# A two-layer hybrid backbone: HGRN's columns first in the input projection, its recurrence beside RWKV's columns

## The chip, the cores and the metric

The kernel runs on one NeuronCore of a Trainium2 chip. Its engines have a queue each: TensorE (PE, with its weight loads PEld), VectorE (DVE), ScalarE (ACT), GpSimd (POOL) and SyncE (SP), which issues most of the DMAs. Matrix products land in PSUM, everything else lies in SBUF. The metric is the device time of one execution in microseconds.

## The reference

One sample of 512 latent tokens and 256 context tokens, model width 1024, two layers. A layer normalises, projects all tokens to the columns of four mixers, joins their outputs in one projection, and ends in a feed-forward block (dense in layer 0, top 2 of 8 experts in layer 1). Cut to the mixers of this change:

```python
h = rms_norm(x) * (1 + scale) + shift
p_hgrn, p_rwkv, p_swa, p_mla = split_cols(h @ w_in[l], GROUP_COLS)

# HGRN2, both directions; chunks of 64 tokens, state S per head
q, zf, zb, i, g = split_cols(p_hgrn, (256,) * 5)
f = lb[d] + (1 - lb[d]) * sigmoid(z);  key = (1 - lb[d]) * sigmoid(-z)
def step(S, inp):                       # gla_chunked, one chunk
    inter = (q * exp(b)) @ S            # b: running sum of log f in the chunk
    att[t, s] = sum_k q[t, k] * key[s, k] * exp(b[t, k] - b[s, k])   # s <= t
    o = inter + att @ i
    S = exp(b_end) * S + (key * exp(b_end - b)).T @ i

# RWKV-7, both directions, a step per token
sa = S @ kk_t
S = S * w_t - sa * b_t + v_t * k_t;  o_t = S @ r_t
```

Each direction starts with the context tokens and goes on over the latents. In layer 1 the context's outputs are not needed.

## The kernel before

The function `mixers` is traced once for each layer and has the stages that matter here.

*Input projection.* The normalised tokens `hhi`, `hlo` (768 tokens, channels on partitions) are multiplied by 23 tiles of 128 columns and by a token-major group (`proj_tok`). Every product takes three passes of split float32 operands (lines 272 to 274). The weights of half a column come by DMA into `raww` and are split by ACT (`hiw`) and DVE (`low`). A column is accumulated in one of three PSUM tiles `big`. The order of the columns is written out: the nine of RWKV (`RW_COLS`) first, then `rw_prep` (decays, keys, values: everything that needs no state, with small products in two PSUM banks `sml`), then HGRN's eight columns, its gates (`hg_gates`), `proj_tok`, and six columns of the attentions, which are spilled to DRAM (`spill`). Ahead of the last three of these `rw_first` prepares the operands of RWKV's first pair of chunks.

*Recurrences.* Python generators are traced side by side by `weave`, which takes a given number of steps of each in turn: `rw_dir` for RWKV's two directions (1 step a round each), `hgrn` for both directions of HGRN (0.44 steps in layer 0, 0.36 in layer 1), `attention_prep` (0.5), and in layer 0 modulation vectors. There are some 122 rounds. RWKV works on pairs of 64-token chunks, six pairs to a direction: `rw_pair` makes their operands (AR, BK), the masked products G and the inverse of a triangular matrix by doubling (TU, TP, AP), and `rw_chain` carries the state Z. HGRN works on segments of four chunks, three to a direction: a segment scales keys and queries by decays (dd, XQ, QE), makes its products level by level into `att`, carries the state `sa`, and writes its output, all through two PSUM banks `hg`. When HGRN's first direction is done, `attention_prep` loads the spilled columns over its inputs.

A list scheduler orders the instructions of each engine by their priority in this trace; memory comes from pools, and a tile of a pool that opens later waits for the one whose place it takes.

Of the kernel before, what the change touches and what calls it, by code (L numbers as in the profile page):

```python
# [23 lines left out]
T = LAT + CTX  # L24
# [10 lines left out]
# columns of the per-layer parameter block  # L35
# [4 lines left out]
# columns of the constant block  # L40
# [7 lines left out]
def _consts():  # L48
    """Constants that depend on shapes alone."""
# [54 lines left out]
def _col_tiles():  # L104
    """Column tiles (lists of w_in columns) that are computed channels x tokens, and the token-major group."""
# [17 lines left out]
# heads 0, 2, 1, 3  # L123
# [6 lines left out]
def _pack(inp):  # L130
# [7 lines left out]
    # shifts and scales of two channel tiles side by side  # L138
# [84 lines left out]
class Ker:  # L223
# [19 lines left out]
    def weave(*gens):  # L243
        """Traces several streams side by side: (generator, steps at a time)."""
# [31 lines left out]
    def gemm_col(s, ps, parts, act, segs):  # L276
        """ps[:, tokens] = weights^T act for one tile of 128 output channels.  parts: (first k, tiles) of the weights."""
# [7 lines left out]
    def gemm_last(s, m, *a):  # L285
        """Column m; the last one a segment after the other, as the norm of the first begins beside the second."""
# [3 lines left out]
    def gemm_cols(s, cols, act, ks=range(KT)):  # L290
        """The same for several column tiles (psum, parts, segments) together, k by k."""
# [8 lines left out]
    def diag(s, out, lhsT, rhs, start=True, stop=True):  # L300
        """64 x 64 products of the two partition halves, each with its own half."""
# [3 lines left out]
    def dtrans(s, out, x, idm):  # L305
        """64 x 64 transposes of the two partition halves."""
# [35 lines left out]
    def setup(s):  # L342
# [5 lines left out]
        s.cst = per.tile([128, C_MSK], F32, name="cst")  # L348
        s.prm = per.tile([128, L, NPRM], F32, name="prm")
        s.cT = per.tile([128, KT, 2], F32, name="cT")  # L350
        s.mskf = per.tile([128, 2, 6, 64], F32, name="mskf")
# [9 lines left out]
        s.mg = s.cst[:, C_MG:C_MG + 512].rearrange("p (d q n) -> p d q n", d=2, q=2)  # L361
# [17 lines left out]
    def setup_masks(s):  # L379
        """The constants that the recurrences need."""  # L380
        Q, V = s.Q, s.V
        Q.dma_start(s.cst[:, C_BO:], s.I['cst'][:, C_BO:C_MSK])
        for l in range(1, L):
            Q.dma_start(s.prm[:, l], s.I['prm'][l])
        Q.dma_start(s.mskf, s.I['cst'][:, C_MSK:C_MSK + 768].rearrange("p (d h n) -> p d h n", d=2, h=6))
        V.tensor_copy(s.msk, s.mskf)
        V.tensor_add(s.id2, s.idn[:, :64], s.idn[:, 64:])
        # masks of the pairs that hold the diagonal as well
        mdf = s.acc[:, :128].rearrange("p (d n) -> p d n", d=2)
        for d in range(2):  # L390
            V.tensor_add(mdf[:, d], s.mskf[:, 1 - d, 0], s.id2)
        V.tensor_copy(s.mdg, mdf)

# [1577 lines left out]
```

## Time and profile before

| | |
|---|---|
| median of 3 runs | 2641.1 us (2638.34 to 2641.53) |
| span of the profiled execution | 2644.5 us; its own time isn't listed beside it, and the span stands 0.13% above the median |
| mean granted TensorE clock | 0.961 of full speed |
| PE, DVE, ACT, POOL busy | 91%, 63%, 46%, 18% of the span |
| layer 0: projection, recurrences | 63 to 288.6 us, 288.6 to 580.2 us |
| layer 1: projection, recurrences | 1395 to 1599 us, 1599 to 1847 us |

The four stretches are those that the change touches; the rest of the span is the norms, the mixers' readout, the output projection and the feed-forward blocks. A busy share of an engine is told by stage, as the stages have different limits. PEclk is the TensorE clock that the throttle granted.

### The profile page before, as it was taken

The numbers are of one execution on the slowest core, as the hardware profiler recorded it, in microseconds if no ns is written. First come the engines' busy times: TensorE is split into PE (matmuls) and PEld (weight loads), VectorE is DVE, ScalarE is ACT, GpSimd is POOL, SyncE is SP. The second block draws the span as 40 slices with busy tenths as digits, with TensorE's granted clock in tenths as the row PEclk, the third lists the DMA queues.
The fourth block names the chain that finished last, engine by engine and source line by source line (L and its number), as shares of the span: only waits on it lengthen the run. The fifth ranks groups of instructions, "written<-read, shape, count | busy, mean of one in ns | idle before, by whom it ended". The sixth has DMA issues, their size and how long they took to land. (4 is left out here: it accounts for less than half of the span.)

```text
span 2644.5 us, 46379 instructions
## 1 busy us (share of the span) xinstructions
PE 2408.1 (91%) x18131; PEld 1998.6 (76%) x18131; DVE 1660.6 (63%) x3055; ACT 1227.3 (46%) x2331; POOL 484.9 (18%) x613
## 2 busy tenths in 40 slices
PE   6999788879998999999999997888996999999994
PEld 3889666656586888888888786666674898899993
DVE  5573598777578644344336746876745667667765
ACT  4373356546723211211234654664653556555653
POOL 1010464441011000000020005654102000000002
PEclk9999899989998999999999998998998899999997
DMA  6223110111053433334322130001113888888885
GB/s 245 65 89 111 49 34 20 30 65 57 1 178 129 144 112 120 117 116 132 118 81 64 57 116 13 20 16 49 56 36 107 267 270 270 280 265 264 260 277 179
DMA packets 161026, 322.46 MB, mean 122 GB/s; under 512 B 12288, under 2 KB 84736, under 8 KB 160800
## 3 DMA queue, kind: packets, MB, share of 16 engines
q1 hardware_dynamic: 153744, 293.60, 34.2%
q0 software_dynamic: 6480, 23.73, 2.5%
q8 instruction: 144, 2.36, 0.4%
q10 hardware_dynamic: 576, 2.10, 0.2%
q14 instruction: 82, 0.67, 0.1%
HBM read 295.39 MB, written 22.54 MB: 120 GB/s over the span
## 5 line engine op out<-in xcount | busy, mean ns | idle before, releaser
L272 PE MATMUL big<-hhi,hiw 128*128 128x512 f32 (+1 forms) x1504 | 520.8, 347 | 9.1 <-ACT hhi L491 4.6
L273 PE MATMUL big<-hlo,hiw 128*128 128x512 f32 (+1 forms) x1504 | 523.6, 348 | 2.4 <-DVE hlo L492 2.4
L274 PE MATMUL big<-hhi,low 128*128 128x512 f32 (+1 forms) x1504 | 519.5, 346 | 5.8 <-DVE low L260 3.9
L259 ACT CAST hiw<-raww 128x512 fp32r<-128x512 f32 (+3 forms) x208 | 158.4, 769 | 616.9 <-PE big L273 413.4
L272 PEld LDWEIGHTS big<-hhi,hiw 128*128 128x128 f32 x1504 | 286.2, 191 | 53.2 <-ACT hhi L491 5.7
L274 PEld LDWEIGHTS big<-hhi,low 128*128 128x128 f32 x1504 | 286.2, 190 | 45.1 <-DVE low L260 5.6
L273 PEld LDWEIGHTS big<-hlo,hiw 128*128 128x128 f32 x1504 | 286.4, 190 | 41.0 <-DVE hlo L492 4.2
L260 DVE TENSOR_TENSOR lom<-rawm,him 128x1024 fp32r<-128x1024 f32 x176 | 215.1, 1225 | 128.0 <-ACT him L259 126.7
L260 DVE TENSOR_TENSOR low<-raww,hiw 128x512 fp32r<-128x512 f32 (+3 forms) x196 | 177.3, 909 | 161.1 <-ACT hiw L259 160.8
L259 ACT CAST him<-rawm 128x1024 fp32r<-128x1024 f32 x176 | 184.3, 1047 | 150.4 <-PE sml L273 60.7
L272 PE MATMUL sml<-xh,him 128*128 128x256 f32 x528 | 152.0, 288 | 0.0
L273 PE MATMUL sml<-xl,him 128*128 128x256 f32 x528 | 149.5, 283 | 0.0
L274 PE MATMUL sml<-xh,lom 128*128 128x256 f32 x528 | 149.4, 283 | 0.0
L260 DVE TENSOR_TENSOR lov<-rawv,hiv 128x1024 fp32r<-128x1024 f32 x88 | 107.5, 1222 | 38.2 <-ACT hiv L259 37.8
L272 PE MATMUL sml<-him,xh 128*128 128x256 f32 x440 | 127.4, 290 | 0.7 <-DVE xl L260 0.6
L273 PE MATMUL sml<-lom,xh 128*128 128x256 f32 x440 | 125.4, 285 | 0.0
L274 PE MATMUL sml<-him,xl 128*128 128x256 f32 x440 | 125.3, 285 | 0.0
L273 PE MATMUL big<-gl,hiw 128*128 128x512 f32 (+1 forms) x352 | 119.5, 339 | 0.0
L272 PE MATMUL big<-gh,hiw 128*128 128x512 f32 (+1 forms) x352 | 118.9, 338 | 0.0
L274 PE MATMUL big<-gh,low 128*128 128x512 f32 (+1 forms) x352 | 118.2, 336 | 0.0
L259 ACT CAST hiv<-rawv 128x1024 fp32r<-128x1024 f32 x88 | 92.4, 1050 | 51.3 <-PE y L274 41.5
L757 POOL TENSOR_TENSOR Gm<-G,mskf 128x256 f32<-128x256 f32 x120 | 99.5, 836 | 85.7 <-PE a L612 82.5
(560 smaller groups left out, 5633.7 us busy)
## 6 DMA issues: line engine op xcount, KB each, us to landing
rawm<-in_m SPq DMA_DIRECT2D x176, 512.0 KB, 5.1
rawv<-in_m SPq DMA_DIRECT2D x88, 512.0 KB, 4.7
raww<-in_wadt SPq DMA_DIRECT2D x56, 512.0 KB, 3.5
raww<-in_w SPq DMA_DIRECT2D x52, 512.0 KB, 3.9
raww<-in_winc SPq DMA_DIRECT2D x92, 256.0 KB, 2.8
raww<-in_wout SPq DMA_DIRECT2D x16, 512.0 KB, 4.1
wadt<-in_wadt SPq DMA_DIRECT2D x16, 512.0 KB, 4.4
raww<-in_w SPq DMA_DIRECT2D x16, 448.0 KB, 3.3
```

What stands on the lines that cost most here:

```text
L259: s.S.copy(hi, src)
L260: (eng or s.V).tensor_sub(lo, src, hi)
L272: s.E.matmul(out, ah, bh, start=start, stop=False)
L273: s.E.matmul(out, ah, bl, start=False, stop=False)
L274: s.E.matmul(out, al, bh, start=False, stop=stop)
L757: P.tensor_mul(x, G[:, :, 0, :, 0], s.mskf[:, 1 - d, i][:, None, None].to_broadcast(sh))
```

## The change

HGRN's columns (11, 12, 13 first, then 14, 9, 10, 15, 16) are projected first, then its gates and `proj_tok`. The generator `hgrn` now exists ahead of the projection's other columns. A new generator `columns` yields after each of RWKV's nine columns, at seven places of `rw_prep` and after each of the six attention columns, 22 times in all, and `weave_while` takes 1.2 steps of HGRN for each. What is left of HGRN is woven into the recurrences at 0.25 steps a round. What goes with it: `sml` shares HGRN's two PSUM banks (`hps`); the weights have 4 and 3 buffers where they had 6 and 4; `rw_first` is gone, and RWKV's first operands are made in a pool that opens behind the projection; RWKV's values go through DRAM (`vts`, `vd`, back to `rwvt`); and RWKV's masks are loaded anew at the start of each layer's recurrences.

```diff
+    HGA, HGB = 1.2, 0.25
+    @staticmethod
+    def weave_while(main, side, n):
+        at = 0.0
+        for _ in main:
+            at += n
+            while at >= 1:
+                at -= 1
+                next(side, None)
...
     def sml(s):
-        return s.ps("sml", 512, s.nsml)
+        return s.ps("sml", 512, s.nsml) if s.nsml else s.hps()
+    def hps(s):
+        return s.ph.tile([128, 512], F32, name="hg", bufs=2)
...
-        return [(4 * q, s.load_split(s.wp, s.I['winc'][l, i, :, 4 * q:4 * q + 4], [128, 4, 128], "w", 6, 4, eng)) for q in qs]
+        return [(4 * q, s.load_split(s.wp, s.I['winc'][l, i, :, 4 * q:4 * q + 4], [128, 4, 128], "w", 4, 3, eng)) for q in qs]
...
     def rw_prep(s, l, last, g, tp):
...
-            s.pad(vt[:, 4 * c4:4 * c4 + 4], pv.rearrange("p c (h n) -> p c h n", h=2), 3)
+            x = tp.tile([128, 512], F32, name="vts", bufs=1)
+            S.copy(x, ps)
+            s.Q.dma_start(vd[:, c4], x)
+        yield
...
-    def rw_first(s, last, g, tp):
-        z = {'AR': s.zeroed(tp, [128, 2, 2, 2, 2, 64], "ARf")[0]}
-        pair = s.rw_pair(0, min(FWD_CH[:2]), last, g, tp, z)
-        next(pair)
-        return z, pair
...
+                hgen = s.hgrn(last, hq, hz, hk, it, hgt, hw)
...
-                        w0 = [s.proj_load(l, i, (0,)) for i in s.RW_COLS[:3]]
+                        COLS = (11, 12, 13)
+                        w0 = [s.proj_load(l, i, (0,)) for i in COLS]
...
+                        def columns():
+                            yield from s.rw_project(l, last, g)
+                            yield from s.rw_prep(l, last, g, s.wp)
...
+                            for i in range(3):
+                                n = LAT if last and i < 2 else T
+                                spill(9 + i, s.proj(l, [(17 + i, n)])[0], n)
+                                yield
+                            for i in range(3):
+                                n = LAT if last and i == 0 else T
+                                spill(5 + i, s.proj(l, [(20 + i, n)])[0], n)
+                                yield
+                        s.weave_while(columns(), hgen, s.HGA)
...
+                    s.mskf = tp.tile([128, 2, 6, 64], F32, name="mskf")
+                    mg = tp.tile([128, 512], F32, name="mg")
...
+                    Q.dma_start(mg, s.I['cst'][:, C_MG:C_MG + 512])
+                    Q.dma_start(s.mskf, s.I['cst'][:, C_MSK:C_MSK + 768].rearrange("p (d h n) -> p d h n", d=2, h=6))
+                    for t in range(2):
+                        h = slice(64 * t, 64 * t + 64)
+                        P.memset(vt[h, :, :, 1 - t], 0.0)
+                        Q.dma_start(vt[h, :, :, t], s.vd[h].rearrange("p c (h n) -> p c h n", h=2))
-                    s.weave(*((s.rw_dir(d, last, g, rwt, *done, bp, tp, ARs, None if d else first), 1) for d in range(2)),
-                            (s.hgrn(last, hq, hz, hk, it, hgt, tp), 0.36 if last else 0.44), (attention_prep(psf), 0.5), *modulation(tp))
+                    s.weave(*((s.rw_dir(d, last, g, rwt, *done, bp, tp, ARs), 1) for d in range(2)),
+                            (hgen, s.HGB), (attention_prep(s.hps), 0.5), *modulation(tp))
```

Three places show how the instructions move, all in layer 0. The first is PE in `rw_prep`: `sml<-xm,acc` (line 338) is one of its small products, `big` the column beside it. Before:

```order
L272 MATMUL big<-hhi,hiw 128x256
L273 MATMUL big<-hlo,hiw 128x256
L274 MATMUL big<-hhi,low 128x256
L338 MATMUL sml<-xm_66,acc 128x512
L338 MATMUL sml<-xm_66,acc 128x256
L272 MATMUL big<-hhi,hiw 128x512
L273 MATMUL big<-hlo,hiw 128x512
L274 MATMUL big<-hhi,low 128x512
L338 MATMUL sml<-xm_66,acc 128x512
L338 MATMUL sml<-xm_66,acc 128x256
L272 MATMUL big<-hhi,hiw 128x256
L273 MATMUL big<-hlo,hiw 128x256
```

Now the same products go to `hg`, where a step of HGRN has its turn ahead of them (`hg<-QE,dd`, `hg<-XQ,dd`, one level of a segment each):

```order
L287 MATMUL big<-hhi,low 128x256
L285 MATMUL big<-hhi,hiw 128x512
L634 MATMUL hg<-QE_1204,dd 64x128 x8
L634 MATMUL hg<-XQ_1202,dd 64x64 x8
L286 MATMUL big<-hlo,hiw 128x512
L287 MATMUL big<-hhi,low 128x512
L355 MATMUL hg<-xm_67,acc 128x512
L285 MATMUL big<-hhi,hiw 128x256
L355 MATMUL hg<-xm_67,acc 128x256
L286 MATMUL big<-hlo,hiw 128x256
L287 MATMUL big<-hhi,low 128x256
```

So products of HGRN and of `rw_prep` stand in a row on the same two banks, in the middle of a column.

The second place is ACT beside it: `rwc` are RWKV's decays (a sigmoid), `dd` HGRN's scaled decays (an exponential). Before:

```order
L537 ACTIVATE xm_67<-big,rwc_128 128x768
L560 ACT_TABLE_LOAD
L560 ACTIVATE rwc_114<-sml,prm 128x512
L560 ACTIVATE rwc_114<-sml,prm 128x256
L560 ACTIVATE rwc_114<-sml,prm 128x512
L560 ACTIVATE rwc_114<-sml,prm 128x256
L560 ACTIVATE rwc_115<-sml,prm 128x512
L560 ACTIVATE rwc_115<-sml,prm 128x256
L567 ACTIVATE xm_67<-xm_67 128x768
```

Now, with an ACT_TABLE_LOAD at each change of function:

```order
L576 ACT_TABLE_LOAD
L576 ACTIVATE rwc_120<-hg,prm 128x512
L576 ACTIVATE rwc_120<-hg,prm 128x256
L584 ACTIVATE rwyg<-rwyg 128x768
L1005 ACT_TABLE_LOAD
L1005 ACTIVATE dd<-dd 128x128x2
L576 ACT_TABLE_LOAD
L576 ACTIVATE rwc_120<-hg,prm 128x512
L576 ACTIVATE rwc_120<-hg,prm 128x256
L1006 ACT_TABLE_LOAD
L1006 ACTIVATE dd<-dd 128x128x2
L981 COPY ket<-hg 128x512
```

The sigmoids stood together behind one load; now exponentials of HGRN come between them.

The third place is DVE at the seam of projection and recurrences: the `COPY` is the last spilled column, G the first masked product of RWKV. Before:

```order
L260 TENSOR_TENSOR low<-raww,hiw 128x512 x6
L1378 COPY xm_65<-big 128x768 x2
L636 MEMSET Z_2259 128x128
L952 MEMSET sa 128x128
L962 TENSOR_TENSOR dd<-hz_101 128x2x4x64
L975 MEMSET att 128x512
L727 TENSOR_TENSOR G<-a_2268,cst 128x512
L727 TENSOR_TENSOR G<-a_2274,cst 128x512
```

Now:

```order
L1385 COPY xm_67<-big 128x768
L1025 COPY_PREDICATED att<-msk,hg 128x8x32
L651 MEMSET Z_2723 128x128
L720 TENSOR_TENSOR BK_2737<-Wi,rwb 128x2x2x64
L725 TENSOR_TENSOR AR_2712<-W,rwkk 64x4x63 x2
L1038 TENSOR_TENSOR sa<-sa,hg 128x128
L651 MEMSET Z_2872 128x128
L999 TENSOR_TENSOR dd<-dd,xm_69 128x512
L720 TENSOR_TENSOR BK_2889<-Wi,rwb 128x2x2x64
L1038 TENSOR_TENSOR sa<-sa,hg 128x128
L738 TENSOR_TENSOR G<-a_2747,mg 128x512
```

BK and AR of RWKV's first pair now stand behind the last column's copy, among the tail of an HGRN segment (`att`, `sa`, `dd`); before they were done ahead of the last three columns.

## Rows read from the trace of the kernel before

**Rows 1.** The page: the span, and a DMA issue with its KB and us to landing.
```profile
span 2644.5 us, 46379 instructions
...
raww<-in_winc SPq DMA_DIRECT2D x92, 256.0 KB, 2.8
```

**Rows 2.** Windows of the four stages: us, then busy us (xinstructions) of each engine, clock, DMA.
```profile
63.00:288.60 225.60, 220.53 (x1229) 188.98 (x1228) 111.92 (x160) 101.42 (x149) 20.00 (x30) 0.99 0.26 86
288.60:580.20 291.60, 235.79 (x3361) 178.63 (x3360) 245.06 (x582) 157.81 (x450) 154.05 (x215) 0.92 0.10 33
1395.00:1599.00 204.00, 201.76 (x1055) 169.11 (x1053) 116.77 (x167) 102.97 (x156) 16.23 (x24) 1.00 0.25 79
1599.00:1847.00 248.00, 203.72 (x2899) 156.70 (x2897) 196.93 (x506) 142.65 (x413) 140.94 (x204) 0.93 0.07 20
```

**Rows 3.** Timeline at the end of layer 0's projection: start, us, engine, instruction, idle before.
```profile
288.33 0.28 PE L274 MATMUL big<-hhi,low 128*128 128x256 f32 x1
...
289.80 1.73 PE L612 MATMUL a<-ARf,BK 128*64 128x256 f32 x14 [1.20 <-DVE xm L1378]
...
290.94 0.68 DVE L727 TENSOR_TENSOR G<-a,cst 128x512 f32<-128x512 f32 x1
```

**Rows 4.** Windows of both recurrences, instructions of tile dd alone.
```profile
288.60:580.20 291.60, 37.31 (x600) 28.58 (x600) 100.57 (x148) 36.13 (x81) 14.54 (x11) 0.92 0.10 33
1599.00:1847.00 248.00, 29.74 (x408) 22.20 (x408) 63.14 (x101) 25.36 (x56) 12.68 (x9) 0.93 0.07 20
```

**Rows 5.** The same, tile att.
```profile
288.60:580.20 291.60, 11.70 (x96) 6.76 (x96) 21.99 (x42) 0.92 0.10 33
1599.00:1847.00 248.00, 8.52 (x64) 4.89 (x64) 14.69 (x28) 0.93 0.07 20
```

**Rows 6.** The same, tile sa.
```profile
288.60:580.20 291.60, 11.45 (x192) 10.39 (x192) 7.20 (x26) 11.79 (x24) 0.92 0.10 33
1599.00:1847.00 248.00, 8.95 (x128) 7.51 (x128) 7.11 (x26) 12.58 (x24) 0.93 0.07 20
```

**Rows 7.** Timeline of PE in layer 1's recurrences: products of an HGRN segment.
```profile
1602.53 0.66 PE L312 MATMUL hg<-cst,dd 128*128 128x128 f32 x4 [0.32 <-DVE dd L964]
...
1605.18 1.09 PE L612 MATMUL hg<-it,ket 128*64 128x128 f32 x16
...
1808.19 0.69 PE L612 MATMUL hg<-XQ,dd 128*64 128x64 f32 x16
...
1815.73 0.46 PE L1037 MATMUL hg<-sa,QE 128*64 128x64 f32 x8
...
1817.14 0.45 PE L1037 MATMUL hg<-sa,QE 128*64 128x64 f32 x8
1817.37 0.28 PE L612 MATMUL c<-rwvt,bkt 128*64 128x128 f32 x1
```

**Rows 8.** Timeline of PE: one channel tile of a 768-token column to the next.
```profile
1590.49 0.39 PE L272 MATMUL big<-hhi,hiw 128*128 128x512 f32 x1
...
1591.55 0.39 PE L272 MATMUL big<-hhi,hiw 128*128 128x512 f32 x1
```

**Rows 9.** Timeline of ACT: a table load and the instruction behind it.
```profile
568.46 1.28 ACT L851 ACT_TABLE_LOAD   x1
569.75 0.31 ACT L851 ACTIVATE rr<-rr,epsc 128x24 f32<-128x24 f32 x1
```

**Rows 10.** Timeline of DVE: two levels of the inverse, late in layer 1's recurrences.
```profile
1828.87 0.29 DVE L781 TENSOR_TENSOR TU<-a,TU 128x128 f32<-128x128 f32 x1 [0.25 <-issue]
...
1832.79 0.29 DVE L781 TENSOR_TENSOR TU<-a,TU 128x128 f32<-128x128 f32 x1 [0.17 <-PE a L612]
```

**Rows 11.** Windows: the stretch of `rw_prep` in layer 0.
```profile
128.00:175.00 47.00, 46.12 (x255) 35.27 (x256) 37.90 (x40) 27.13 (x38) 11.26 (x19) 1.00 0.28 93
```

**Rows 12.** Timeline of PE: one group of its small products.
```profile
128.85 1.56 PE L338 MATMUL sml<-xm,acc 128*128 128x512 f32 x4 [1.41 <-ACT rwc L560]
```

**Rows 13.** Windows: first and last stretch of the recurrences, layers 0 and 1.
```profile
290.00:330.00 40.00, 27.78 (x313) 20.06 (x310) 35.08 (x68) 19.41 (x53) 24.55 (x36) 0.79 0.14 49
1818.00:1848.00 30.00, 23.07 (x241) 15.90 (x241) 16.21 (x41) 10.50 (x30) 10.36 (x11) 0.78 0.14 46
```

More of the change, by code (lines that the diff above doesn't have):

```diff
@@ L523, with rw_project @@
     RW_COLS = (6, 7, 2, 3, 4, 5, 0, 1, 8)
-    def rw_project(s, l, last, g, pss):
+    def rw_project(s, l, last, g):
         V, S = s.V, s.S
@@ L532, in rw_project @@
         dst = [g[n][:, j] for n in 'rkv' for j in range(2)] + [g['yw'], g['ya'], g['yg']]
-        cols = [(i, LAT if last and i in (0, 1, 8) else T) for i in s.RW_COLS]
-        for n in range(0, 9):
-            (i, ntok), ps = cols[n], pss[n] if n < 3 else s.proj(l, cols[n:n + 1], s.P if n == 3 else None)[0]
+        for i in s.RW_COLS:
+            ntok = LAT if last and i in (0, 1, 8) else T
+            ps, = s.proj(l, [(i, ntok)])
             d = dst[i]
@@ L620, in zeroed, with rw_dir @@
         return r
-    def rw_first(s, last, g, tp):
-        z = {'AR': s.zeroed(tp, [128, 2, 2, 2, 2, 64], "ARf")[0]}
-        pair = s.rw_pair(0, min(FWD_CH[:2]), last, g, tp, z)
-        next(pair)
-        return z, pair
-    def rw_dir(s, d, last, g, O, done, both, t0, tp, ARs, first=None):
+    def rw_dir(s, d, last, g, O, done, both, t0, tp, ARs):
         V = s.V
@@ L647, in prep @@
         def prep(i):
-            if first and i == 0:
-                zi, pair = first
-                zi.update(z)
-                return zi, (yield from pair)
             a = (2 * i + d) % 3
@@ L935, in hgrn @@
         done = set()
-        def psh():
-            return s.ps("hg", 512, 2)
+        psh = s.hps
         def ch4(x):
@@ L1293, in mixers @@
             s.sk = hp.tile([128, 4], F32, name="sk")
-            with s.pool("rec", side="right") as rp:
+            with ExitStack() as rx:
+                rp = rx.enter_context(s.pool("rec", side="right"))
+                s.ph = rx.enter_context(s.pool("ph", 1, PSUM))
+                hw = rx.enter_context(s.pool("hw", side="right"))
                 g = {}
@@ L1340, in mixers @@
                             if a == 1:
-                                w1 = [s.proj_load(l, i, (1,), P) for i in s.RW_COLS[:3]]
+                                w1 = [s.proj_load(l, i, (1,), P) for i in COLS]
                             if a < 3:
@@ L1354, in mixers @@
                             gemm(w1, range(6, KT), (j,))
-                        s.rw_project(l, last, g, pss)
-                        for x in (g['vt'], it):
-                            for t in range(2):
-                                P.memset(x[64 * t:64 * t + 64, :, :, 1 - t], 0.0)
-                        s.rw_prep(l, last, g, s.wp)
-                        if l == 0:
-                            s.clear_rows()
-                        P.dma_start(gd[:, 4, :nq], g['yg'][:, :nq])
-                        for t in range(2):
-                            for p in range(2):
-                                P.dma_start(gd[64 * t:64 * t + 64, 2 + p, :nq], g['v'][64 * p:64 * p + 64, t, :nq])
-                        for i in range(2, 6):
-                            ps, = s.proj(l, [(9 + i, T)])
-                            (S.copy if i % 2 else V.tensor_copy)(hz[i // 2 - 1][:, i % 2], ps[:, :T])
+                        for i in range(2, 6):
+                            ps = pss[i - 2] if i < 5 else s.proj(l, [(9 + i, T)])[0]
+                            (S.copy if i % 2 else V.tensor_copy)(hz[i // 2 - 1][:, i % 2], ps[:, :T])
+                        for t in range(2):
+                            P.memset(it[64 * t:64 * t + 64, :, :, 1 - t], 0.0)
                         nb = 0
@@ L1389, in mixers @@
                         P.dma_start(gd[:, 8], rwo[:, 1])
-                        for i in range(3):
-                            n = LAT if last and i < 2 else T
-                            spill(9 + i, s.proj(l, [(17 + i, n)])[0], n)
-                        first = s.rw_first(last, g, bp)
-                        for i in range(3):
-                            n = LAT if last and i == 0 else T
-                            spill(5 + i, s.proj(l, [(20 + i, n)])[0], n)
-                hgt, rwt = (x.rearrange("p a (c n) -> p (a c n)", n=64).rearrange(tok, c=12, t=2) for x in (hgo, rwo))
+                        def columns():
+                            yield from s.rw_project(l, last, g)
+                            yield from s.rw_prep(l, last, g, s.wp)
+                            if l == 0:
+                                s.clear_rows()
+                            P.dma_start(gd[:, 4, :nq], g['yg'][:, :nq])
+                            for t in range(2):
+                                for p in range(2):
+                                    P.dma_start(gd[64 * t:64 * t + 64, 2 + p, :nq], g['v'][64 * p:64 * p + 64, t, :nq])
+                            for i in range(3):
+                                n = LAT if last and i < 2 else T
+                                spill(9 + i, s.proj(l, [(17 + i, n)])[0], n)
+                                yield
+                            for i in range(3):
+                                n = LAT if last and i == 0 else T
+                                spill(5 + i, s.proj(l, [(20 + i, n)])[0], n)
+                                yield
+                        s.weave_while(columns(), hgen, s.HGA)
+                bp = wx.enter_context(s.pool("b0"))
                 def modulation(tp):
```

59 lines of the change are left out of this document (30 added, 29 removed).

## The prediction

> **What bounds the kernel now.** I read the page first: one core, a span of 2644.5 us [rows 1]. Then I cut the two layers' mixers into their stages [rows 2]. In the input projection TensorE (PE) is busy 220.53 of 225.60 us in layer 0 and 201.76 of 204.00 in layer 1, while VectorE (DVE) has about half of the stretch free, ScalarE (ACT) too. So whatever is added to PE there lengthens the stage by its own time, and whatever is added to DVE or ACT is free as long as PE need not wait for it. The recurrences are the other way: DVE is busy 245.06 of 291.60 us (84%) in layer 0 and 196.93 of 248.00 (79%) in layer 1; PE has 81% and 82%. Neither is full: the chains hop between engines. One comparison gives the worth of a microsecond of DVE there. Both layers run the same RWKV recurrence, layer 1 with a smaller HGRN share: 48.13 us less DVE go with 43.60 us less time [rows 2], 0.91 us each. The seam between the stages is short: the last column's product starts at 288.33, the first of RWKV's at 289.80, its mask on DVE at 290.94 [rows 3].
>
> The HGRN share I read from its three tiles that carry nearly all of its DVE work: dd 100.57, att 21.99 and sa 7.20 us in layer 0, together 129.76; in layer 1 63.14, 14.69 and 7.11, together 84.94 [rows 4 to 6].
>
> **The change, part by part.** At 1.2 steps for each of the 22 yields, 26 HGRN steps are traced in the projection. Layer 0 has 55 steps (1 and then 6 segments of 9), so the forward direction moves but for the end of its last segment. Layer 1 has 41, since its two context segments have 2 each; the forward direction and five steps of the backward one move.
>
> *A. HGRN's products on a full PE.* A segment is, in rows [rows 7]: the turn of the keys 0.66, the state product 1.09, five levels at 0.69, a sixth, double-width one that I put at the state product's 1.09, and the output block, 1815.73 to 1817.59, of which I count 1.64 up to the next product at 1817.37. Sum 7.93 us. Layer 0 moves three: 23.8. Layer 1 moves a context segment (0.66 + 1.09 = 1.75), two whole ones (15.9), another context segment (1.75) and the start of one (0.66 + 1.09 + 0.69 = 2.44): 21.8. PE had 5.1 and 2.2 us free there, not enough to hide any of it safely. Together **+45.6**, at best +38.
>
> *B. Waits of PE inside the projection.* Beside RWKV's nine columns I cost them at nothing: each step of HGRN stands behind a column of 8 × 1.06 = 8.5 us [rows 8], and its few DVE and ACT instructions fit in that. Beside `rw_prep` it is tighter. Its small products and HGRN's now take turns in two PSUM banks, where `rw_prep` had two of its own; its work used to be followed by more than ten columns of cover and is followed by six (51 us); and ACT now alternates between sigmoid and exponential, which reloads its function table. The order of after holds 75 loads against 55 before. A load is 1.28 us, and the next ACT instruction follows at 569.75, 1.29 after the load's start [rows 9]. Twenty switches are 26 us of ACT for both layers. ACT has room for them, and they hurt only where a bank stays full meanwhile. Ends 0 and 26; I take half, **+13**, since big columns stand between most of the small products but not between all.
> By the Trainium skill ("ScalarE: Activation LUTs", What ACT_TABLE_LOAD costs) a switch is the load and a drain behind it, about 2.66 us in all, and functions should be kept together by table; by that the twenty switches would be 53 us, B 27 and the sum below -4. The trace agrees with the load and shows no drain behind it, so I keep 1.29.
>
> *C. A later start of RWKV.* The first pair's operands are no longer prepared under the last three columns. Behind the last product come the copy of the last column, the operands BK and AR on DVE, and only then the product; the masks and the values also come by DMA into memory that the projection leaves, on SP's queue behind a transfer that waits for HGRN's forward half. What is queued behind them on DVE are the tail steps of HGRN, and PE waits for both. The old seam is 288.33 to 290.94, 2.6 us [rows 3]; I take that once more per layer: **+6**. Ends 0 (the scheduler starts BK early) and 12 (the masks' DMA, two more seams' worth).
>
> *D. Fewer weight buffers* (four of six). Two columns' weights are still held; a half column lands in 2.8 us [rows 1] and a column computes for 8.5, so the prefetch covers it but for the first columns, where the norm starts late. **+4**, ends 0 and 8. The values' trip through DRAM replaces six DVE copies by three of ACT; that, the masks kept out of constants and GpSimd's lost split are at nothing, under DVE's and ACT's free halves of the projection; uncovered, they would be some 2 us.
>
> *E. The recurrences without half of HGRN.* Layer 0 loses half of 129.76, 64.9 us of DVE; by the 0.91 that is -59. The other end goes by PE: 235.79 less 23.8, at the share of 82%, is 258.5, or -33. Layer 1 loses 42.5 and about 7 for the five steps, 49.5 us; ends -45 and, by PE (203.72 less 21.8 over 0.82), -26. RWKV's own floor lies below this: a level of its inverse takes 3.92 us, 1828.87 to 1832.79, with little beside it [rows 10]; five are 20, and with products, mask and transposes ahead I estimate 28 to 30 us for a pair, against a mean of 48.6 and 41.3 now (six pairs to a direction). In layer 1 HGRN's 15 steps at 0.25 end in the middle of the stage, and the second half runs against this floor. DVE is the fuller engine in layer 0, so I go near its end: **-50**; in layer 1 the middle: **-37**.
>
> Sum: 45.6 + 13 + 6 + 4 - 87 = **-18**, on 2644.5 gives 2626. The median of the runs shown lies 3.4 us under that execution, so 2623 is the time I predict.
>
> **Rivals.** (1) *All of it comes off.* The 0.91 holds in both layers (-104), no bank stalls, C 3 and D 0: -55, some 2586. For it: DVE's 84%; against: PE at 81% is next in line at once.
>
> (2) *`rw_prep` is the new bound, and the kernel is slower.* The stretch 128 to 175, which holds `rw_prep` before, has 37.90 us of DVE [rows 11] under 46 us of PE work. After, the 13 yields from here to the end of the projection bring some 16 HGRN steps: 16/9 of a segment's 21.6 us (129.76 over six), 38 of DVE. With ten table switches (13) and a dozen hand-offs at 1.20, the wait seen in [rows 3], the chain is 37.9 + 38 + 13 + 14 = 103 us. PE has 51 of columns, 14 of HGRN and ten groups of small products of about 1.5 [rows 12], together 80. If all these run in one chain PE waits 23 us per layer: B is 46 for 13, +15 in sum, 2656. It decides from some 18 us of waiting per layer. For it: two banks for three users, strict order on DVE. Against: the three big banks let PE run ahead of DVE by up to three columns, 25 us.
>
> (3) *The clock takes it back.* The granted clock of PE is 0.79 at the start of the recurrences, 290 to 330, and 0.78 at their end [rows 13], where PE is busy for 69% and 77%, against 0.99 and 1.00 in the projections [rows 2]. With HGRN's products gone PE idles more. If both stages went from 0.92 and 0.93 to 0.79, PE's 212 and 182 us would be 35 and 32 longer; a third of that on the path is +22, 2645. Against: in the stage as a whole PE's share should hold, since time shrinks too.
> The Trainium skill ("TensorE: Matmul & The Clock Gate", HAM oscillation) says that PE, when it idles between bursts of matmuls, falls back to its slow clock again and again. The two stretches at 0.79 and 0.78 agree with that.
>
> **Chances.** The forecast 0.42, with 2605 to 2635 as its own range; (1) 0.18; (2) 0.20; (3) 0.20. What a measurement can tell from no change is 0.2%, 5.3 us. Faster: nearly all of the forecast, (1), a little of (3): 0.58. Slower: (2) and the upper part of (3): 0.27. The same: 0.15. The range goes from just under rival (1) to just over rival (2), 2582 to 2660.
>
> **What would show it.** Right: projections longer by about 23 to 35 us each with PE still near 95% busy; recurrences near 242 and 211 us; DVE in them near 180 and 147. B shows as PE idle released by ACT or DVE on the small banks between the ninth RWKV column and the last six; C as the time from the last column's product to RWKV's first mask. The prediction is wrong if the projection shows long idle stretches of PE behind `rw_prep` (2), if the granted clock of the recurrences falls below 0.85 (3), or if the recurrences lose less than DVE's half of HGRN would say, because the chain of hops, not DVE, sets them.

## The result: 0.5% slower, and the profile after

The changed kernel takes 2654.7 us (median of 5 runs, 2649.8 to 2659.0) where the kernel before takes 2640.3 (5 runs): a ratio of 1.0054, with an interval of 1.0039 to 1.0068. The forecast was 2623; the sign was wrong.

The profiled execution has a span of 2657.2 us, 12.7 more than that of [rows 1]. On the page of the changed kernel VectorE has a little less work than before (1653.0 us, 1660.6 before), and PE is busy 21 us longer (2408.1 before) for the same 18131 matmuls:

```profile
span 2657.2 us, 46488 instructions
...
PE 2429.0 (91%) x18131; PEld 2003.0 (75%) x18131; DVE 1653.0 (62%) x3053; ACT 1252.3 (47%) x2351; POOL 469.1 (18%) x609
```

The four stages of the changed kernel, which answer to [rows 2] (us, then busy us and instructions of PE, PEld, DVE, ACT, POOL, then the granted clock and the DMA's share):

```profile
63.00:319.00 256.00, 246.52 (x1649) 207.84 (x1648) 161.09 (x257) 139.77 (x210) 33.28 (x41) 0.98 0.26 82
319.00:574.20 255.20, 213.56 (x2950) 158.89 (x2949) 187.86 (x481) 136.82 (x405) 138.94 (x210) 0.93 0.14 40
1388.00:1623.30 235.30, 227.49 (x1437) 185.71 (x1437) 160.20 (x257) 132.19 (x209) 38.77 (x47) 0.99 0.25 78
1623.30:1855.00 231.70, 190.59 (x2509) 143.10 (x2509) 152.68 (x412) 122.25 (x367) 120.03 (x186) 0.90 0.10 24
```

Both projections have grown, by 30.4 and 31.3 us. Both recurrences have shrunk, by 36.4 and 16.3 us. Counted so, with the seam in the recurrences, the exchange gains 6 us in layer 0 and loses 15 in layer 1. DVE's work in the recurrences fell by 57.2 and 44.3 us. It is now busy for 74% and 66% of them, so it has room there, and the stage shrank by less than its work.

The seam, which answers to [rows 3]: the end of the projection in layer 0 of the changed kernel (start, us, engine, instruction, idle time before it).

```profile
318.81 0.28 PE L287 MATMUL big<-hhi,low 128*128 128x256 f32 x1
...
319.16 0.94 POOL L640 MEMSET AR<- 128x1024 f32 x1 [5.01 <-PE big L287]
...
320.05 2.80 POOL L1469 MEMSET rwvt<- 64x1536 f32 x2
...
325.60 0.72 POOL L728 TENSOR_TENSOR AR<-W,rwr 64x256 f32<-64x256 f32 x1
...
326.38 0.29 PEld L634 LDWEIGHTS a<-AR,BK 128*64 128x64 f32 x4 [3.99 <-POOL AR L728]
326.38 3.25 PE L634 MATMUL a<-AR,BK 128*64 128x256 f32 x13 [3.75 <-POOL AR L728]
...
328.40 0.69 DVE L738 TENSOR_TENSOR G<-a,mg 128x512 f32<-128x512 f32 x1 [1.27 <-PE a L634]
```

The last column's product starts at 318.81, RWKV's first at 326.38, its mask at 328.40. GpSimd stands between: it zeroes AR, then for 2.80 us the unused halves of the values, and only then makes its part of BK and AR. The seam takes 9.3 us from the end of the last product to the first mask where it took 2.3; in layer 1 it is 7.6 where it was 1.9.

For all kernels below I read the same three lengths from the trace: the projection (first product of a column to the end of the last), the seam, and the recurrences (first mask to the end of the chain's last product). Layer 0 is ahead of the slash and layer 1 behind it; a ratio is taken against runs of the kernel before on the same chip. Each length is of one profiled execution: e1 and f2, which differ at the seam alone, have 243.2 and 247.2 us for the recurrences of layer 1, so a difference of 4 us there says little.

| kernel | projection | seam | recurrences | median, us | ratio to before |
|---|---|---|---|---|---|
| before | 259.8 / 213.8 | 2.3 / 1.9 | 288.9 / 245.5 | 2640.3 | |
| changed | 290.2 / 245.1 | 9.3 / 7.6 | 245.4 / 223.7 | 2654.7 | 1.0054 (1.0039 to 1.0068) |
| e1, none beside | 255.0 / 215.5 | 10.2 / 7.2 | 272.6 / 243.2 | 2639.1 | 0.9991 (0.9982 to 1.0001) |
| e2, rest left out | 292.5 / 237.6 | 9.5 / 7.6 | 220.5 / 207.7 | | |
| e3, zeros late | 290.3 / 244.9 | 7.3 / 4.9 | 250.6 / 233.5 | 2661.9 | 1.0076 (1.0055 to 1.0098) |
| e4, layer 0 only | 289.4 / 216.0 | 9.3 / 7.2 | 243.2 / 243.2 | 2647.2 | 1.0028 (1.0016 to 1.0040) |
| e5, fill | 290.9 / 247.1 | 14.3 / 11.8 | 253.5 / 224.0 | 2668.7 | 1.0097 (1.0074 to 1.0120) |
| e6, none beside, fill | 254.6 / 215.3 | 14.4 / 11.5 | 282.0 / 250.6 | 2663.1 | 1.0074 (1.0047 to 1.0102) |
| e7, before with fill | 258.5 / 213.5 | 2.3 / 1.9 | 295.1 / 250.9 | 2665.2 | 1.0091 (1.0069 to 1.0113) |
| e8, e6 with zeros late | 254.6 / 215.5 | 20.1 / 11.8 | 282.6 / 255.6 | 2675.1 | 1.0130 (1.0107 to 1.0152) |
| f1, zeros by DMA | 289.4 / 245.4 | 7.3 / 4.9 | 246.4 / 224.2 | 2651.3 | 1.0042 (1.0026 to 1.0059) |
| f2, e1 with zeros by DMA | 254.7 / 215.4 | 8.2 / 5.0 | 273.7 / 247.2 | 2636.5 | 0.9985 (0.9975 to 0.9995) |
| f3, columns only | 277.6 / 236.4 | 9.7 / 9.9 | 244.8 / 217.6 | 2629.6 | 0.9965 (0.9952 to 0.9978) |
| g1, tangents | 290.2 / 242.3 | 9.3 / 7.6 | 245.2 / 220.2 | 2649.5 | 1.0040 (1.0023 to 1.0057) |
| g2, f3 with zeros by DMA | 277.9 / 237.1 | 9.6 / 7.5 | 252.3 / 223.4 | 2642.4 | 1.0013 (0.9998 to 1.0028) |
| g3, g2 with tangents | 278.4 / 235.3 | 9.6 / 7.5 | 248.9 / 227.4 | 2639.0 | 1.0000 (0.9987 to 1.0012) |

### The profile page after: what moved, and what is told of

Same layout as the page of the kernel before. It is cut to its first block, busy times and chain, and to the rows that moved or that the text cites. A ratio compares the mean times of both kernels' runs of the same rounds, so it can differ in the third digit from the quotient of the medians.

```text
span 2657.2 us, 46488 instructions
## 1 busy us (share of the span) xinstructions
PE 2429.0 (91%) x18131; PEld 2003.0 (75%) x18131; DVE 1653.0 (62%) x3053; ACT 1252.3 (47%) x2351; POOL 469.1 (18%) x609
## 5 line engine op out<-in xcount | busy, mean ns | idle before, releaser
L273 POOL TENSOR_TENSOR low<-raww,hiw 128x512 fp32r<-128x512 f32 (+1 forms) x8 | 13.4, 1690 | 574.6 <-ACT hiw L272 533.1
```

The lines of the kernel that those rows point to most:

```text
L273: (eng or s.V).tensor_sub(lo, src, hi)
```

## The experiments

### What the moved steps cost and give

e1 keeps the new order of the columns, the shared banks, the buffers and the seam, and puts no HGRN step beside the projection:

```diff
-                        s.weave_while(columns(), hgen, s.HGA)
+                        s.weave_while(columns(), hgen, 0)
...
-                            (hgen, s.HGB), (attention_prep(s.hps), 0.5), *modulation(tp))
+                            (hgen, 0.36 if last else 0.44), (attention_prep(s.hps), 0.5), *modulation(tp))
```

> The changed kernel with no HGRN step beside the projection and the old 0.44 and 0.36 steps a round in the recurrences; the order of the columns, the shared banks, the fewer buffers and the new seam stay. Theory F (RWKV's own chain of hops is the floor of the recurrences, so HGRN's work there costs less the less of it is left): the projections come back to some 226 to 232 and 214 to 219 us, the recurrences from their first mask are as in the kernel before (289 and 245 us), and the seams keep their 9.3 and 7.6 us; in all 2652 to 2660 us. Rival S (what was lost is the price of steps beside the projection, stalls above all): the time falls to 2641 or below.

It takes 2639.1 us, the time of the kernel before and within what rival S had: the 15 us are lost by the moved steps, and the rest of the change is worth nothing in sum. The projection of layer 1 and the seams came near what theory F had. Layer 0's projection is shorter: from 63 us on, as in [rows 2], it takes 221.4 us where F had 226 to 232. F's total was 13 us too high at its lower end mainly because the recurrences of layer 0 take 272.6 us here and not 289. Windows of e1's recurrences, from the first mask on:

```profile
294.40:566.90 272.50, 224.52 (x3318) 168.58 (x3314) 226.24 (x559) 153.86 (x439) 148.76 (x208) 0.96 0.10 33
1593.50:1836.70 243.20, 195.68 (x2860) 150.48 (x2856) 195.87 (x492) 141.68 (x407) 143.42 (x203) 0.94 0.08 20
```

The granted clock is 0.96 in layer 0, where [rows 2] has 0.92. What else in the old stage cost layer 0 some 16 us I have not taken apart.

e2 is the changed kernel without those HGRN segments that have not begun when the projection ends. It leaves out the backward direction in layer 0 and the last segment of it in layer 1, so tokens go to other experts, and its total is not read.

```diff
+                if s.skip:
+                    if want and sg in done:
+                        V.memset(s.rr[0][:, 4 * sg:4 * sg + 4], 1.0)
+                    elif want:
+                        V.memset(O[:, 4 * sg:4 * sg + 4], 0.0)
+                        done.add(sg)
+                    continue
...
                         s.weave_while(columns(), hgen, s.HGA)
+                        s.skip = True
```

> The changed kernel that leaves out the HGRN segments which have not begun when the projection ends (its output is not the reference's). Theory F: the recurrences from their first mask still take about 210 us or more in layer 1 (224 now) and about 215 in layer 0 (245 now). Rival D (a microsecond of VectorE is still worth 0.91 us, and something else in the new recurrences took the gain): the 34 and 65 us of HGRN's VectorE work that are left come off at 0.91, so 193 and 186 us.

The windows of its recurrences:

```profile
331.70:552.20 220.50, 191.64 (x2390) 139.61 (x2386) 122.85 (x360) 112.92 (x347) 104.56 (x165) 0.93 0.09 32
1610.20:1817.90 207.70, 176.84 (x2308) 133.41 (x2304) 123.42 (x361) 113.15 (x344) 105.83 (x167) 0.92 0.07 18
```

220.5 and 207.7 us: near theory F's 215 and 210, and far from the 186 and 193 of rival D. With nearly no HGRN there, DVE is busy for 56% and 59% of the stage, and the stage still takes 90% and 93% of what it takes in the changed kernel. What is left is RWKV's own work, with the attentions' preparation beside it. That its chain of hops between the engines sets the length is argued and not shown: PE is busy for 87% and 85% of these windows, more than in any of the other recurrences above, and no run takes work of RWKV off PE.

e1 and e2 now give the price of HGRN in the recurrences. The largest of its three tiles, dd, in e1's windows:

```profile
294.40:566.90 272.50, 32.90 (x564) 25.62 (x564) 87.02 (x134) 31.80 (x72) 14.59 (x10) 0.96 0.10 33
1593.50:1836.70 243.20, 26.91 (x400) 20.61 (x400) 64.23 (x95) 23.14 (x52) 11.33 (x8) 0.94 0.08 20
```

With att (20.03 and 14.17) and sa (7.00 and 6.40), the tiles of [rows 4 to 6] have 114.1 and 84.8 us of DVE in e1; they have 0.7 and 6.8 in e2 (the segment that had begun in layer 1 runs on). Between the two the stages differ by 52.1 and 35.5 us, which is 0.46 us for each of DVE in either layer, or 0.50 and 0.49 by all that DVE does there. That is a mean. The part that the change moves, from e1 to the changed kernel, brings 27.2 us (272.6 to 245.4) and 19.5 (243.2 to 223.7), 0.54 and 0.36 for each of DVE; the part that is left there is worth 0.40 and 0.68. So the price is not lower for the last part in both layers, as theory F's reason would have it.

e4 moves HGRN's steps in layer 0 alone:

```diff
-                        s.weave_while(columns(), hgen, s.HGA)
+                        s.weave_while(columns(), hgen, 0 if last else s.HGA)
...
-                            (hgen, s.HGB), (attention_prep(s.hps), 0.5), *modulation(tp))
+                            (hgen, 0.36 if last else s.HGB), (attention_prep(s.hps), 0.5), *modulation(tp))
```

> HGRN beside the projection in layer 0 alone; layer 1 has the old 0.36 steps a round in the recurrences. Theory F: layer 1's projection gives back some 28 us, its recurrences take 22 back; 6 us less than the changed kernel, 2648. Theory S or D: layer 1 gives back 28 and takes 45, so 2671.

2647.2 us, as theory F had it, half-way between e1 and the changed kernel: each layer's move loses some 8 us.

### Where the projection's waits come from

In the changed kernel PE stands idle mainly in one place of layer 0's projection, behind `rw_prep`. Windows of 10 us there:

```profile
259.00:269.00 10.00, 10.00 (x98) 7.88 (x97) 9.90 (x9) 4.07 (x6) 0.72 (x1) 1.00 0.18 67
269.00:279.00 10.00, 4.11 (x24) 1.79 (x22) 9.94 (x16) 5.10 (x8) 2.40 (x4) 0.80 0.34 132
279.00:289.00 10.00, 9.45 (x81) 6.81 (x82) 6.83 (x13) 1.88 (x3) 3.40 (x7) 0.68 0.58 159
```

DVE is full in the first two slices (9.90 and 9.94 of 10 us). PE still has products in the first and idles for 5.9 us in the second. The granted clock, 1.00 until then, goes to 0.80 and then 0.68, and PE is slow in the third slice although it has work again. The view of waits names the releaser, XQ, an operand that DVE makes for HGRN (us in total, times, longest):

```profile
PE hg L634 <- DVE XQ L1010: 7.0, 3, 2.9
```

f3 has the same 26 steps beside the projection, but none inside `rw_prep`:

```diff
-    HGA, HGB = 1.2, 0.25
+    HGA, HGB = 1.75, 0.25
...
-                            yield from s.rw_prep(l, last, g, s.wp)
+                            for _ in s.rw_prep(l, last, g, s.wp):
+                                pass
```

> The changed kernel with as many HGRN steps beside the projection (26), 1.75 for each column and none inside the stretch that prepares RWKV. Theory B (TensorE's 9 and 4 us of idle time in that part of the projection come of HGRN's steps and RWKV's preparation sharing VectorE and two banks): TensorE's idle time there falls below 2 us, each projection is 4 to 8 us shorter, 2643 to 2648. Rival Q (VectorE has that much to do in the last third anyway): the idle time only moves, and the time is within 3 us of the changed kernel's.

It takes 2629.6 us, 25 less than the changed kernel, which is more than theory B had; it is under the kernel before too, by 0.35%. The slices behind its `rw_prep`:

```profile
248.60:258.60 10.00, 10.00 (x84) 7.88 (x82) 10.00 (x7) 3.27 (x6) 0.72 (x1) 1.00 0.17 66
258.60:268.60 10.00, 10.00 (x56) 8.27 (x53) 8.38 (x10) 2.40 (x4) 1.24 (x3) 1.00 0.36 120
268.60:278.60 10.00, 9.88 (x124) 7.79 (x123) 7.76 (x17) 6.13 (x9) 4.72 (x9) 1.00 0.63 199
```

DVE has as much to do (10.00 in the first slice), and PE waits for 0.1 us and keeps its clock. Rival Q falls: PE has columns to work on there while DVE is full, and no product of HGRN that waits for DVE. The projections are 12.6 and 8.7 us shorter.

g1 asks whether ACT's table loads made the waits. It leaves all steps where the change has them and writes RWKV's sigmoids by the hyperbolic tangent, which shares the exponential's table; 75 table loads become 51.

```diff
-        S.activation(g['yg'][:, :nq], g['yg'][:, :nq], AF.Sigmoid)
+        S.activation(g['yg'][:, :nq], g['yg'][:, :nq], AF.Tanh, scale=0.5)
+        S.activation(g['yg'][:, :nq], g['yg'][:, :nq], AF.Copy, bias=0.5, scale=0.5)
```

> The changed kernel with RWKV's sigmoids written as half of a hyperbolic tangent and a half, a function that shares the exponential's table: 51 table loads in all and not 75, with seven more copies of 768 columns on ScalarE in each layer, some 6 us; the steps of HGRN keep their places. Theory T (the table loads make the waits): each projection gets 8 to 12 us shorter, 2632 to 2640. Rival Q (VectorE's queue and the two banks make them): the projections stay within 3 us, 2652 to 2656.

The projection of layer 0 stays at 290.2 us and that of layer 1 loses 2.8; the median, 2649.5, is 5 us lower and lies between the two forecasts, with 3.5 us of it in layer 1's recurrences. For the projections theory T falls. ACT has less to do in this stretch, but DVE has as much, and PE still idles in small pieces and loses its clock. The three slices in which it idles most, which are not neighbours:

```profile
236.60:246.60 10.00, 8.92 (x35) 5.30 (x36) 5.95 (x13) 5.94 (x9) 0.31 (x1) 0.66 0.17 58
266.60:276.60 10.00, 7.72 (x66) 5.48 (x68) 9.33 (x17) 2.51 (x5) 2.69 (x4) 1.00 0.35 106
286.60:296.60 10.00, 8.37 (x52) 7.31 (x53) 6.45 (x13) 2.15 (x6) 1.30 (x2) 0.83 0.10 39
```

The releasers that the view of waits names there are DVE's again, XQ and an `att` (us in total, times, longest):

```profile
PE hg L639 <- DVE XQ L1015: 4.0, 2, 2.3
PE hg L355 <- DVE att L1030: 1.9, 1, 1.9
```

So PE waits for what DVE makes. The clock is lower in two of the three slices (0.66 and 0.83) and full in the one at 266.6 us, which has the most idle time. Whether more than two banks would also have helped was not tried.

### The seam

e3 makes the zeros of the values depend on the masks, so that GpSimd takes them up later:

```diff
-                        P.memset(vt[h, :, :, 1 - t], 0.0)
+                        P.tensor_scalar_mul(vt[h, :, :, 1 - t], s.mskf[h].rearrange("p d h n -> p (d h) n")[:, :, None].to_broadcast([64, 12, 2, 64]), 0.0)
```

> GpSimd zeroes the unused halves of RWKV's values only when the masks have come, behind the first pair's operands and not ahead of them. Theory P (GpSimd's queue is what holds the first product at the seam): the first mask comes 2.8 us earlier in each layer, in all 5 to 6 us off. Rival M (the masks' and values' DMA sets the start of the recurrences): the first mask moves but the later pairs don't, and the time stays within 2 us of the changed kernel's.

The seams lose 2.0 and 2.7 us, and the time grows by 7. It doesn't answer its question, because the replacement was itself dear: two multiplications of 4.2 us on GpSimd where two memsets took 2.80 together, right ahead of the first pair's TT.

```profile
324.58 8.39 POOL L1469 TENSOR_SCALAR rwvt<-mskf 64x1536 f32<-64x1536 f32 x2
```

f1 takes the zeros from DRAM rows that are zero already:

```diff
-                        P.memset(vt[h, :, :, 1 - t], 0.0)
                         Q.dma_start(vt[h, :, :, t], s.vd[h].rearrange("p c (h n) -> p c h n", h=2))
+                    for t in range(2):
+                        h = slice(64 * t, 64 * t + 64)
+                        for i in range(2):
+                            Q.dma_start(vt[h, :, i, 1 - t], s.yb[128 * s.NB:128 * s.NB + 64, :768].rearrange("p (c n) -> p c n", n=64))
```

> The changed kernel whose zeros in RWKV's values come by DMA, so that GpSimd's queue at the seam loses the two memsets of 1.4 us and gets nothing in their place. Theory P (GpSimd's queue holds the first product): the first mask 2 to 3 us earlier in each layer and the later pairs too, 4 to 6 us under the changed kernel. Rival M (the values' DMA sets the pace of the first pair): the first mask is earlier, the values later, and the time is the same or longer.

The seams lose 2.0 and 2.7 us again, the recurrences keep their length within 1 us, and the median is 3.4 us lower. That lies between theory P's 4 to 6 us and rival M's none, and the intervals of the two ratios overlap. f2 is the same edit on e1:

> The same with no HGRN step beside the projection (0.44 and 0.36 steps in the recurrences). Theory P: 4 to 6 us under the 2639 of that version, 2633 to 2635, a little under the kernel before. Rival M: 2639 or more.

2636.5 us, 2.6 less than e1, again between the two forecasts and with intervals that overlap. The seams show 4.7 us less in all, of the 12.7 that they have grown by; the two medians put the memsets at some 3 us, which is not clear of the noise in either pair.

### The clock at the start of the recurrences

e5 fills PE's idle time with matmuls that nobody reads:

```diff
+                    def warm():
+                        for n in (3, 3, 3) + (1,) * 20:
+                            ps = s.hps()
+                            for _ in range(n):
+                                s.E.matmul(ps, s.idn, s.cst[:, 0:512], start=True, stop=True)
+                            if n == 1:
+                                yield
...
-                            (hgen, s.HGB), (attention_prep(s.hps), 0.5), *modulation(tp))
+                            (hgen, s.HGB), (attention_prep(s.hps), 0.5), (warm(), 1), *modulation(tp))
```

> The changed kernel with 29 matmuls of 128x512 whose result nobody reads: nine or so at the seam, the others one a round behind it, some 20 to 25 us of TensorE per layer where it was 30 to 75% busy. Theory K (the idle seam lets TensorE's granted clock fall, and the first pairs of the recurrences run at the lower level): the granted clock of the first 50 us rises from some 0.6 to above 0.9, the first period of a pair falls from 41 and 36 us to 35 and 31, and the kernel gains 6 to 15 us, 2640 to 2649. Rival O (the first pairs are held by hops between the engines at any clock): the clock rises, the periods stay or grow, and the time is the changed kernel's or up to 10 us longer.

The first 50 us of the recurrences in the changed kernel, layer 0 and layer 1:

```profile
328.10:378.10 50.00, 40.91 (x442) 28.16 (x438) 35.02 (x85) 28.37 (x72) 26.73 (x43) 0.88 0.27 90
1630.60:1680.60 50.00, 42.41 (x486) 34.22 (x484) 32.18 (x88) 27.58 (x73) 25.38 (x44) 0.74 0.14 33
```

and with the fill:

```profile
334.30:384.30 50.00, 44.59 (x387) 26.65 (x388) 27.02 (x65) 20.37 (x56) 20.50 (x29) 0.93 0.05 15
1652.20:1702.20 50.00, 46.72 (x492) 30.22 (x491) 26.22 (x80) 27.09 (x66) 20.52 (x34) 0.97 0.06 15
```

The granted clock goes from 0.88 and 0.74 to 0.93 and 0.97, and the kernel is 14 us slower (11 by the ratios, which are taken on one chip each). That is more than rival O's 10. The fill was heavier than I had reckoned: each matmul shows as two of 0.59 us, 34 us a layer, and those at the seam stand ahead of RWKV's first product, which puts the first mask 5.0 and 4.2 us later. The first period of a pair doesn't fall (45 and 40 us for 41 and 36). Theory K's gain did not come; that a lighter fill would bring it is not excluded. The fill on e1 and on the kernel before, with the same edit, gave the same answer, and e8 added to it the dear zeros of e3.

> No HGRN step beside the projection, with the same matmuls at the seam. Theory K: 5 to 10 us under the version without them (2639), so 2629 to 2634. Rival O: 2639 or more.

> The kernel before with the same matmuls at its seam. Theory K: its first 40 us had a granted clock of 0.79; that rises above 0.9, and layer 0's recurrences lose part of the 16 us by which they were longer than those of the version without steps beside the projection; 2628 to 2636. Rival O: 2640 or more.

> No HGRN step beside the projection, the matmuls at the seam, and the zeros of the values behind the first pair's operands. Theory K: the 2 us that the seam lost in each layer when only the zeros were moved now stay won, so 3 to 5 us under the version with the matmuls alone. Rival O: the first mask comes earlier, and the end doesn't.

By medians 24 us more than e1, 21 more than the kernel before in the same runs, and 36 more than e1: no gain each time, as rival O had it.

### Do the parts add up?

g2 joins f3 and f1; g3 adds g1's tangents.

> No HGRN step inside RWKV's preparation (2630), and the zeros of the values by DMA, which took 2 to 3 us off the seam of either kernel. If the two are independent: 2626 to 2628, under both kernels by some 0.5%; if the seam is hidden by something else in this order: 2630.

> The same with the sigmoids as tangents. Theory T: the loads that are left in the preparation stand alone, so no more than 2 us off, 2624 to 2628. Rival Q: ScalarE's added copies cost 0 to 3 us, 2626 to 2630.

They don't. g2 takes 2642.4 us (its runs 2632.4 to 2648.7), 13 more than f3. Its projections are f3's within 3 us, and its recurrences are 7.5 and 5.8 us longer. The first 50 us of layer 0's recurrences in g2, with a granted clock of 0.73:

```profile
317.50:367.50 50.00, 40.33 (x370) 28.00 (x370) 31.92 (x75) 25.83 (x66) 23.99 (x36) 0.73 0.29 75
```

and in f3, with 0.93:

```profile
315.80:365.80 50.00, 41.06 (x475) 28.09 (x473) 37.29 (x94) 30.12 (x79) 29.35 (x42) 0.93 0.26 88
```

PE gets 370 matmuls done there for 475, in about the same busy time. Executions of one program differ in the same way: 21 runs of the kernel before, taken beside f3, have mean clocks of 0.962 to 0.968 and times of 2633.1 to 2645.3 us, and the line through them falls by 13.9 us for each 0.01 (correlation -0.76). The changed kernel's five runs have a mean clock of 0.9588 and those 21 have 0.9648; at that slope 0.006 is 8 us of the 14 that were lost. This is an association, overlaps with the terms below, and does not hold everywhere: the ten runs of e1 show no such line (0.4 us, correlation 0.03), and e5 has a higher mean clock than the changed kernel (0.967) and is slower. So the 8 us are not shown. Why the clock stays low longer in one order of instructions than in another is open. So is whether the clock is what costs g2 its 13 us: its zeros land 6.5 us behind layer 0's first mask, and no run parts the two, though f1, with the same edit, lost nothing in its recurrences. f3 is the fastest of these kernels; f2 too lies under the kernel before, by 0.15%.

## Why the prediction was wrong, step by step

**What bounds the stages.** Right for the projection: PE is full (246.52 of 256.00 us in layer 0), and A came out as reckoned. From the end of `proj_tok` to the last product, f3 takes 167.4 and 151.0 us and e1 144.3 and 129.3, so the moved steps cost 23.1 and 21.8 us where 23.8 and 21.8 were predicted.

For the recurrences it was wrong, and this is the step that failed: "One comparison gives the worth of a microsecond of DVE there", 0.91 us. Two layers were compared that differ in more than HGRN. e2 shows that layer 1's stage is 12.8 us shorter with nearly none of it (207.7 to 220.5), and e1 that layer 0's had 16 us in it that had nothing to do with the place of HGRN's steps. Measured by taking the work out, the worth is 0.46 us. At that price the 64.9 and 49.5 us that leave are worth 30 and 23 us, not the 50 and 37 of E. The prediction had named this among its signs of being wrong: recurrences that lose less than DVE's half of HGRN would say.

**E, the recurrences:** -87 predicted, -65.3 measured (288.9 to 245.4 and 245.5 to 223.7), and only -46.7 of that comes of the moved steps (-27.2 and -19.5); the other -18.6 e1 has as well. Layer 0's -43.5 lies in its bounds by luck: the moved steps alone bring less than either end (with layer 0's own PE share of 81% that end is -30). Layer 1's -21.8 lies outside: both its ends, -26 by PE's share and -45 by DVE, took an engine for the bound, and the floor of RWKV, which the text put at 28 to 30 us a pair, was estimated from two rows and is 35 to 37 in e2 (220.5 and 207.7 us over six pairs). That mean has a slow start in it: counting the pairs of masks as the two directions' in turn, the first of a direction stands 35 to 46 us ahead of its second, and from the third on they are 29 to 34 us apart. The work itself did leave the stage as reckoned: DVE's part in dd is 48.70 and 25.81 us in the new one, against the 100.57 and 63.14 of [rows 4].

```profile
319.00:574.20 255.20, 23.33 (x316) 17.84 (x316) 48.70 (x73) 18.54 (x41) 6.94 (x5) 0.93 0.14 40
1623.30:1855.00 231.70, 14.07 (x180) 10.59 (x180) 25.81 (x38) 8.68 (x19) 2.66 (x2) 0.90 0.10 24
```

**B, waits in the projection:** 13 predicted, 21.1 measured (179.9 less 167.4 and 159.6 less 151.0 us, changed kernel against f3, from the end of `proj_tok`). Those windows of the changed kernel, layers 0 and 1:

```profile
139.20:319.10 179.90, 171.16 (x1222) 139.06 (x1223) 117.38 (x189) 82.86 (x130) 29.63 (x37) 0.97 0.25 78
1463.70:1623.30 159.60, 153.07 (x1050) 120.14 (x1051) 108.99 (x178) 77.08 (x129) 33.25 (x41) 0.98 0.22 69
```

and of f3:

```profile
138.90:306.30 167.40, 166.93 (x1207) 136.89 (x1206) 112.46 (x185) 68.24 (x119) 28.66 (x37) 1.00 0.26 84
1449.40:1600.40 151.00, 149.33 (x1034) 118.31 (x1034) 108.32 (x175) 69.60 (x122) 28.97 (x39) 1.00 0.23 74
```

Of the 21.1 us, 13.1 are idle time of PE (8.7 and 6.5 us against 0.5 and 1.7), and 8.0 are a longer busy PE, for 1% to 2% more matmuls and at a granted clock of 0.97 and 0.98 instead of 1.00. That the idle part alone is the forecast 13 is luck. The place was right and the bound of 26 held. The cause was named wrongly: the sum came from table loads, and by g1 they are worth nothing in layer 0's projection and 2 to 3 us in layer 1's. Rival (2) had the mechanism, DVE's chain behind `rw_prep` with columns that no longer cover it, at twice the size; PE idled 9 us and not 23 in layer 0, as it still had products for the first 10 us in which DVE was full. The slow clock behind the idle stretch was in neither.

**C, the seam:** 6 predicted, 12.7 measured, just over its upper end. The chain through DVE was as told; GpSimd's queue, with AR's and the values' zeros ahead of its part of BK and AR, was not in it. The DMA of the masks held nothing: that of mg is issued at 319.16, lands some 4.0 us later, and G begins at 328.40.

**D, fewer buffers:** 4 predicted. No run changes the buffers alone. In e1, which has them with the new order of the columns, the two projections together are 3 us shorter than before (255.0 and 215.5 for 259.8 and 213.8), so no cost of theirs can be seen.

**The sum.** The projections' 61.7 us are A (44.9), B (21.1) and -4.3 for the rest; with C 12.7, E -65.3 and 3.6 outside these stages that makes 12.7, the difference of the two spans. Two terms carry the error: E by 22 us and B with C by 15.

**Rival (3), the clock,** was half right. The recurrences' granted clock is 0.93 and 0.90, so layer 0's did not fall and layer 1's did by 0.03, far from the 0.79 that was priced. The Trainium skill ("TensorE: Matmul & The Clock Gate", HAM oscillation) has PE fall back to its slow clock when it idles between bursts of matmuls. The slices at 269 and 279 us agree with that: 5.9 us of idle time, then a clock of 0.68. In g1 a slice with 2.3 us of idle time kept 1.00.

The other rule of the Trainium skill that was weighed ("ScalarE: Activation LUTs", What ACT_TABLE_LOAD costs) decided nothing, since by g1 the loads were not what PE waited for in layer 0.

## What to carry to other kernels

To price work that is to move from one stage to another, take it out of the first and look, or compare two runs of the same stage; two layers that differ in other things give a slope that isn't the work's. Work that goes beside a full engine should stand where the other engines have room in that very stretch: the same 26 steps cost 21 us less beside plain columns than partly inside a preparation that already filled VectorE. A stage in which no engine is full can have a floor of its own, and that is to be measured by taking work out, ahead of any share of busy time.

## What the runs showed of the hardware

- Idle time of TensorE went with a lower clock: 5.9 us within 10 us came with a granted clock of 0.80 in that slice and 0.68 in the next. Over the whole stretch behind `proj_tok` in layer 0 TensorE idled 8.7 us against 0.5 in f3, and the stretch was 12.5 us longer.
- Executions of one program differ with the mean granted clock: 13.9 us for each 0.01 over 21 runs of the kernel before. Ten runs of e1 did not (0.4 us).
- On GpSimd a multiplication by a constant that wrote 64x1536 from a repeated mask took 4.2 us, a memset of the same shape 1.37 us.
- The fill's float32 matmul of 128x512 showed as two instructions of 0.59 us, a product of the columns of that shape, whose operands the kernel declares float32r, as one of 0.39 [rows 8].
